# Layer norm's loads issued a block ahead, z and the attention heads stored unsplit and split after the load

## The chip, the cores and the metric

The kernel runs on one core of a Trainium2 chip. The metric is the device time of one execution in microseconds. Two runs of the kernel before took 1401.67 and 1411.05 us, median 1406.36 us.

## What is computed

One layer of a streaming encoder block for 1024 positions of width 1024, all in float32:

```python
h = rms_norm(x, g_pre)
glu_in, gate_a, q, k, v, gate_b, merge = split(h @ w_in)
u = causal_depthwise_conv31(glu_a * sigmoid(glu_b)) + conv_b
z = silu(layer_norm(u, ln_g, ln_b)) * silu(gate_a)
y_a = z @ w_conv_proj
w = softmax(q1 k1, chunk mask) - lam * softmax(q2 k2, chunk mask)   # 8 heads
o = rms_norm(w @ v, g_subln) * (1 - lambda_init)
y_b = (o * silu(gate_b)) @ w_attn_proj
y = sigmoid(m_a) * y_a + sigmoid(m_b) * y_b
out = x + rms_norm(y @ w_out, g_post)
```

A float32 product is computed from split operands: each operand is written as a high part (the value cast to the type float32r, on ScalarE, ACT) and a low part (the value less its high part, on VectorE, DVE, or GpSimd, POOL). Three matmuls, high with high, high with low and low with high, are summed in PSUM. "Splitting" below always means this cast and this subtraction.

## The kernel before

Activations lie transposed: 128 channels on the partitions, 1024 positions along the row. So a "block" is 128 x 1024 values (512 KB), and a half of it 128 x 512. Everything that a later stage needs goes through DRAM. Three stages follow one another.

**Projection.** `h @ w_in` is computed in pairs of channel blocks, each pair by seven products of halves (`quarters`, L518; `product`, L236) whose sums and differences give the four quarters of the result. The pairs and the three parts of the layer norm are ordered by hand:

```python
PLAN = ("u0 g0 u1 g1 q0 u2 q1 q2 u3 q3 q4 u4 q5 q6 u5 q7 s0 u6 s1 s2 u7 s3 v0 v1 v2 v3 "
        "m0 m1 l0 g2 l1 l2 m2 g3 m3")
```

The quarters go through up to seven buffers of the tag `cmb` (L533: `u2`, `u3`, `c22`) and six PSUM banks; the `use_` functions consume them. For the pairs m and g that is a tanh on ACT (`tanh_half`, L360) into a tile of the tag `th`, for g also a multiply, and a store. The tag `th` has six buffers (`small`, L321), used by nearly everything in this stage that has half a block.

The layer norm works on the convolved blocks in DRAM (`cv_dram`). Its parts are l0, `ln_squares` (L463): load each block, subtract the mean, store it, sum the squares; l1, `ln_roots` (L479): the inverse roots; l2, `ln_out` (L490): load each centred block (L499), multiply it by the roots (L500, DVE), silu (L501, ACT), and for each half load the gate `ga` (L504), multiply (L505, DVE), split the product (L507 ACT, L508 DVE) and store both parts (L510). Blocks lie in three buffers: two of the tag `u`, one of `cv` (`ln_tile`, L457). The halves (`gaz`, `zh`, `zl`) come from `th`.

**Attention.** Head after head (`head`, L818), in four steps of 256 queries: scores on TensorE (PE), exponentials on ACT (L859), the difference of the two maps on DVE (L868), its transposes on PE (L875), their split on ACT and DVE (L877, L878), and the product with v (L888). Between these, `take(n)` draws n pieces of other matmuls from the generator `filling` (L737): first `merge_gate` for the eight blocks of m_b (64 pieces of 6 matmuls), then `conv_out` (z @ w_conv_proj, 64 pieces of 6), then `attn_out` for the first four heads (32 pieces of 6). How many are drawn at each step is written out in `pieces` (L751). z is loaded when the gates are through (`load_z`, L671), the heads 0 to 3 ahead of `attn_out`, the heads 4 and 5 after head 6 (`load_og`, L811); both on POOL's DMA queue, into 16 block buffers which the projection's input held before (`block`, L619).

`norm_head` (L788) finishes a head: it loads the inverse roots (`orb`, L798), multiplies on POOL (L799), and splits the result (L804 ACT, L805 POOL). The heads below 6 are then stored, high and low (L809). The tiles of half a block in this stage (`orb`, `ogh`, `ogl`, `tar` and `tbr`, `yar`, `th`) share four buffers of the tag `hf` (`halftile`, L614).

**Output.** The last heads' projection, the merge, `y @ w_out` and the norm.

Within an engine and on each DMA queue instructions run in the order that the framework's scheduler fixed when the kernel was built. It goes by the program's order and by its own estimate of when operands and buffers become free. SyncE (SP) issues nearly all the DMAs; an instruction that waits there holds up those behind it.

Of the kernel before, what the change touches and what calls it, by code (L numbers as in the profile page):

```python
# [11 lines left out]
F32 = mybir.dt.float32  # L12
F32R = mybir.dt.float32r
I32 = mybir.dt.int32
AF = mybir.ActivationFunctionType
ALU = mybir.AluOpType
# [8 lines left out]
H = 8  # L25
# [42 lines left out]
def block_kernel(ctx, tc, x, positions, vecs, conv_w, lambdas, g_subln, g_post,  # L68
                 w_in, w_cp, w_ap, w_out, out):
    nc = tc.nc  # L70
# [7 lines left out]
    def rows(name, n, shape=(P, T)):  # L78
        return [dram.tile(list(shape), F32, name=f"{name}{i}") for i in range(n)]
# [4 lines left out]
    sg_dram, ga_dram, ta_dram, tb_dram = rows("sg", 8), rows("ga", 8), rows("ta", 8), rows("tb", 8)  # L84
    cc_dram = rows("cc", 8)
    b12_dram = rows("b12", 4, (P, HALF))
    cv_dram, z_dram, og_dram = rows("cv", 8), (rows("zh", 8), rows("zl", 8)), (rows("ogh", 6), rows("ogl", 6))
    ya_dram, ya2_dram = rows("ya", 8), rows("yab", 8)
    ors_dram = dram.tile([H, T], F32, name="ors_dram")

# [167 lines left out]
    for c, tiles in enumerate(((0, 1, 2, 3), (4, 5, 6, 7))):  # L258
        for t in tiles:
# [6 lines left out]
                                                        op0=ALU.mult, op1=ALU.mult)  # L266
        if c:
            begin_pair()
        for d in (range(8) if c == 0 else (4, 0, 5, 1, 6, 2, 7, 3)):
# [3 lines left out]
            g = vec[:, 0, d:d + 1]  # L273
            if c == 0 or d >= 4:
# [4 lines left out]
                                               op0=ALU.mult, op1=ALU.subtract)  # L279
# [41 lines left out]
    def small(name, dt=F32):  # L321
        return work.tile(hb, dt, name=name, tag="th", bufs=6)
# [140 lines left out]
    def ln_squares():  # L463

        mu = ps.tile(blk, F32, name="mu", tag="cv", bufs=1)
        for sl in halves:
            nc.tensor.matmul(mu[:, sl], ones_d, ln["tot"][:, sl], start=True, stop=True)
        for i in range(8):
            c = ln_tile(i, "cvr")
            nc.sync.dma_start(out=c, in_=cv_dram[i])  # L470
            nc.vector.tensor_tensor(out=c, in0=c, in1=mu, op=ALU.subtract)
            nc.sync.dma_start(out=cc_dram[i], in_=c)
            for sl in halves:
                sq = small("csq") if i else ln["tot"][:, sl]
                nc.scalar.activation(out=sq, in_=c[:, sl], func=AF.Square)
                if i:
                    nc.vector.tensor_tensor(out=ln["tot"][:, sl], in0=ln["tot"][:, sl], in1=sq, op=ALU.add)
# [12 lines left out]
    def ln_out():  # L490
        rs = ps.tile(blk, F32, name="rs", tag="cv", bufs=1)
        for a in range(8):
            dg = small("diag")[:, 0:P]
            nc.vector.tensor_scalar(out=dg, in0=ident, scalar1=ln["r"][:, a:a + 1], scalar2=float(D),
                                    op0=ALU.mult, op1=ALU.mult)
            nc.tensor.matmul(rs[:, a * P:(a + 1) * P], ones_d, dg, start=True, stop=True)
        for i in range(8):
            c = ln_tile(i, "cvz")
            nc.sync.dma_start(out=c, in_=cc_dram[i])  # L499
            nc.vector.tensor_tensor(out=c, in0=c, in1=rs, op=ALU.mult)  # L500
            nc.scalar.activation(out=c, in_=c, func=AF.Silu, scale=vec[:, 2, i:i + 1], bias=vec[:, 3, i:i + 1])  # L501
            for sl in halves:
                g = small("gaz")
                nc.sync.dma_start(out=g, in_=ga_dram[i][:, sl])  # L504
                nc.vector.scalar_tensor_tensor(out=g, in0=c[:, sl], scalar=0.5, in1=g, op0=ALU.mult, op1=ALU.mult)  # L505
                a, b = small("zh", F32R), small("zl", F32R)
                nc.scalar.copy(out=a, in_=g)  # L507
                nc.vector.tensor_tensor(out=b, in0=g, in1=a.bitcast(F32), op=ALU.subtract)  # L508
                for n, t in enumerate((a, b)):
                    nc.sync.dma_start(out=z_dram[n][i][:, sl], in_=t.bitcast(F32))  # L510

    def ln_part(n):
        (ln_squares, ln_roots, ln_out)[n]()
# [100 lines left out]
    def halftile(name="hf", dt=F32):  # L614
        return pools["h"].tile(hb, dt, name=name, tag="hf", bufs=4)
# [3 lines left out]
    def block(name):  # L619

        nblock[0] += 1
        pool, tag, n = (b2pool, "c", 4) if (nblock[0] - 1) % 16 >= 12 else (bpool, "b", 12)
        return pool.tile([P, 2, HALF], F32R, name=name, tag=tag, bufs=n).rearrange("p a b -> p (a b)")
# [44 lines left out]

    zH, zL, ogH, ogL = [], [], [], []

    def load_z(i):  # L671
        a, b = block("zH"), block("zL")
        for n, t in enumerate((a, b)):
            nc.gpsimd.dma_start(out=t.bitcast(F32), in_=z_dram[n][i])
        zH.append(a)
        zL.append(b)

    def psum_g2():
        return ps.tile(hb, F32, name="ps_g", tag="g", bufs=1)
# [39 lines left out]
    def attn_out(i):  # L719

        w = weight(("ap0", i))
        for hh in range(2):
# [11 lines left out]
                load_weight()  # L734
            yield

    def filling():  # L737
        for i in range(8):
            yield from merge_gate(i)
        for i in range(8):  # L740
            load_z(i)
        for i in range(8):
            yield from conv_out(i)
        for i in range(4):
            load_og(i)
        for i in range(8):
            yield from attn_out(i)

    fill = filling()
# [1 line left out]
    def pieces(h, i):  # L751

        if h == 3:
            return 1, int(i >= 4)
        if h == 6:
            return (0, 0) if i == 2 else (1, 1)
        return (1, 1) if h < 3 else (2, 1)
# [30 lines left out]
    def norm_head(h):  # L788

        og = heads.pop(h)  # L790
        if h >= 6:
            a, b = block("ogH"), block("ogL")
            ogH.append(a)
            ogL.append(b)
        for hh in range(2):
            sl = halves[hh]
            rb = halftile("orb")
            nc.sync.dma_start(out=rb, in_=ors_dram[h:h + 1, sl].broadcast_to([P, HALF]))  # L798
            nc.gpsimd.tensor_tensor(out=og[:, sl], in0=og[:, sl], in1=rb, op=ALU.mult)  # L799
            if h < 6:  # L800
                ah, bh = halftile("ogh", F32R), halftile("ogl", F32R)
            else:
                ah, bh = a[:, sl], b[:, sl]
            nc.scalar.copy(out=ah, in_=og[:, sl])  # L804
            (nc.vector if h == 7 else nc.gpsimd).tensor_tensor(  # L805
                out=bh, in0=og[:, sl], in1=ah.bitcast(F32), op=ALU.subtract)
            if h < 6:
                for n, t in enumerate((ah, bh)):
                    nc.sync.dma_start(out=og_dram[n][h][:, sl], in_=t.bitcast(F32))  # L809

    def load_og(h):  # L811
        a, b = block("ogH"), block("ogL")
        for n, t in enumerate((a, b)):
            nc.gpsimd.dma_start(out=t.bitcast(F32), in_=og_dram[n][h])
        ogH.append(a)
        ogL.append(b)

    def head(h, loaded_head):  # L818
        st, vH, vL, sg = loaded_head
# [93 lines left out]
    def norm_row(h):  # L913

        rt = psum_2()
        nc.tensor.transpose(out=rt[0:8, 0:P], in_=roots.pop(h), identity=ident)
        row = side("row")
        nc.scalar.copy(out=row[0:8, 0:P], in_=rt[0:8, 0:P])
        nc.sync.dma_start(out=ors_dram[h:h + 1, :].rearrange("o (a p) -> (o a) p", p=P), in_=row[0:8, 0:P])
# [8 lines left out]
    for h in range(8):  # L928
        nxt = head(h, nxt)
        if h == 6:  # L930
            load_og(4)
            load_og(5)
    norm_row(7)
    norm_head(7)
    for _ in fill:
# [152 lines left out]
```

## Time and profile before

| | |
|---|---|
| Two runs, median | 1401.67 and 1411.05, 1406.36 us |
| The profiled execution, its own time | 1409.51 us |
| Its span, first to last instruction | 1407.4 us |
| Mean granted clock of TensorE | 0.942 |
| Moved by DMA | 237.89 MB |

A row of the tables by stretches gives the start and end in us, the length, the busy us of PE, PEld (weight load), DVE, ACT and POOL with the number of instructions, then TensorE's granted clock, the share of DMA that was busy, and GB/s. A row of a timeline gives start, length, engine, line, operation, the tile written and those read, the shape, the count, and in brackets how long the engine was idle before and what ended this. SPq is SyncE's DMA queue, POOLq GpSimd's. A row of waits gives who waited for whom, the us in total, how often, and the longest. A row of one line's or tile's instructions gives count, shortest, median and longest in ns, and the first and last start. A row of DMA issues ends with the size of each and the median us from issue to landing.

### The profile page before, as it was taken

Reading aid. Unit: us, or ns where it says so; the run is one execution under the profiler, and the core shown is the slowest. Engines: PE = TensorE matmul, PEld = TensorE weight load, DVE = VectorE, ACT = ScalarE, POOL = GpSimd, SP = SyncE. Lnnn points to the kernel's source line nnn. Section 1 sums busy time; section 2 is a strip of 40 time slices with the busy share of each in tenths; the row PEclk is TensorE's granted clock in tenths of the full one; section 3 lists DMA queues with packets and bytes.
Section 4 is the critical chain, followed back from the end, with each engine's and each line's share of the span. In section 5 each row is a group of like instructions: output and inputs, shape, how many; then the busy total and the mean of one; then the engine's idle time right before and its main releaser. Section 6 shows DMA issues by size and latency. Waiting matters only on the chain. (4 is left out here: it accounts for less than half of the span.)

```text
span 1407.4 us, 17086 instructions
## 1 busy us (share of the span) xinstructions
PE 1221.7 (87%) x5700; PEld 1009.3 (72%) x5700; DVE 990.4 (70%) x1561; ACT 528.8 (38%) x1051; POOL 698.1 (50%) x560
## 2 busy tenths in 40 slices
PE   3799999999899999998921699988899889969998
PEld 2578777878788877786810488877778778857786
DVE  4879998998999999639533165676566567836733
ACT  7533342323333333343422254544343335423311
POOL 4798799999888886675500211322221223353000
PEclk9999999999999999999965699998999999989999
DMA  5223444434432244655456956688756676558432
GB/s 206 71 85 110 150 142 157 155 118 154 149 120 91 93 169 142 232 170 200 139 182 214 236 158 182 179 256 284 219 175 195 173 241 205 191 189 266 155 121 86
DMA packets 100279, 237.89 MB, mean 169 GB/s; under 512 B 12016, under 2 KB 12480, under 8 KB 100192
## 3 DMA queue, kind: packets, MB, share of 16 engines
q1 hardware_dynamic: 95360, 219.75, 49.6%
q0 software_dynamic: 4112, 14.83, 2.9%
q10 hardware_dynamic: 720, 2.23, 0.4%
q8 instruction: 45, 0.74, 0.2%
q14 instruction: 42, 0.34, 0.1%
HBM read 157.04 MB, written 79.72 MB: 168 GB/s over the span
## 5 line engine op out<-in xcount | busy, mean ns | idle before, releaser
L241 PE MATMUL ps_g<-T,wf 128*128 128x512 f32 x1536 | 362.3, 392 | 5.8 <-DVE u L525 5.6
L241 PE MATMUL ps_g<-B,wf 128*128 128x512 f32 x1152 | 289.9, 405 | 74.9 <-DVE c L525 70.2
L241 PEld LDWEIGHTS ps_g<-T,wf 128*128 128x128 f32 x1536 | 289.3, 189 | 67.6 <-DVE u L525 5.2
L241 PEld LDWEIGHTS ps_g<-B,wf 128*128 128x128 f32 x1152 | 224.3, 196 | 126.9 <-DVE c L525 73.9
L447 DVE SCALAR_TENSOR_TENSOR cacc<-u,cw,cacc 128x1024 f32<-128x1024 f32 x232 | 297.7, 1283 | 2.9
L182 POOL TENSOR_TENSOR wf<-wraw,wf 128x512 fp32r<-128x512 f32 x128 | 177.4, 1390 | 56.7 <-ACT wf L181 56.7
L644 POOL TENSOR_TENSOR wL<-wraw,wH 128x512 fp32r<-128x512 f32 x44 | 57.8, 1328 | 271.3 <-ACT wH L643 252.5
L182 POOL TENSOR_TENSOR wf<-wsum,wf 128x512 fp32r<-128x512 f32 x96 | 130.0, 1354 | 23.1 <-ACT wf L181 22.8
L859 ACT ACTIVATE e<-ps_s,nm 128x256 f32<-128x256 f32 (+7 forms) x128 | 94.7, 743 | 97.4 <-DVE nm L856 36.4
L181 ACT CAST wf<-wraw 128x512 fp32r<-128x512 f32 x128 | 78.2, 617 | 98.3 <-PE ps_g L241 80.5
L709 PE MATMUL ps_g<-B,wH 128*128 128x512 f32 x256 | 87.4, 423 | 18.5 <-ACT wH L643 13.2
L181 ACT CAST wf<-wsum 128x512 fp32r<-128x512 f32 x96 | 59.3, 618 | 87.5 <-POOL wsum L203 44.4
L525 DVE SCALAR_TENSOR_TENSOR u<-ps_g,u 128x512 f32<-128x512 f32 x96 | 65.6, 684 | 37.3 <-PE ps_g L241 37.1
L846 PE MATMUL ps_s<-kst,qh 128*128 128x384 f32 (+4 forms) x192 | 69.5, 370 | 5.8 <-ACT e L859 5.8
L878 DVE TENSOR_TENSOR wtL<-ps_r,wtH 128x512 fp32r<-128x512 f32 (+2 forms) x96 | 52.1, 549 | 30.3 <-ACT wtH L877 29.8
L709 PEld LDWEIGHTS ps_g<-B,wH 128*128 128x128 f32 x256 | 50.8, 204 | 30.4 <-ACT wH L643 13.9
L847 PE MATMUL ps_s<-kst,ql 128*128 128x384 f32 (+4 forms) x192 | 66.5, 354 | 1.0 <-DMA ql<-qkl 1.0
L856 DVE TENSOR_REDUCE nm<-ps_s 128x1 f32<-128x640 f32 (+3 forms) x64 | 65.1, 1018 | 0.9
L799 POOL TENSOR_TENSOR og<-og,orb 128x512 f32<-128x512 f32 x16 | 20.5, 1281 | 84.6 <-DMA orb<-ors_dram 59.2
L666 PE MATMUL ps_g<-zH,wH 128*128 128x512 f32 x128 | 53.2, 416 | 9.5 <-DVE tar L692 9.5
L203 POOL TENSOR_TENSOR wsum<-wraw 128x512 f32<-128x512 f32 x32 | 43.7, 1365 | 35.9 <-DMA wraw<-w_in 33.6
L877 ACT CAST wtH<-ps_r 128x512 fp32r<-128x512 f32 (+2 forms) x96 | 44.7, 479 | 39.5 <-PE ps_r L875 39.0
(227 smaller groups left out, 2360.4 us busy)
## 6 DMA issues: line engine op xcount, KB each, us to landing
wraw<-w_in SPq DMA_DIRECT2D x67, 512.0 KB, 3.7
qkh<-qkH SPq DMA_DIRECT2D x32, 256.0 KB, 2.3
qkl<-qkL SPq DMA_DIRECT2D x32, 256.0 KB, 2.0
qh<-qkh SPq DMA_DIRECT2D x32, 256.0 KB, 7.8
ql<-qkl SPq DMA_DIRECT2D x32, 256.0 KB, 8.4
tbr<-tb SPq DMA_DIRECT2D x32, 256.0 KB, 2.9
sg<-th SPq DMA_DIRECT2D x16, 256.0 KB, 5.0
cv<-cv SPq DMA_DIRECT2D x8, 512.0 KB, 4.0
```

Source lines behind the costliest of these rows:

```text
L181: nc.scalar.copy(out=f[:, 0, :], in_=src)
L182: nc.gpsimd.tensor_tensor(out=f[:, 1, :], in0=src, in1=f.bitcast(F32)[:, 0, :], op=ALU.subtract)
L241: nc.tensor.matmul(acc, f[:, l, sl], b[:, r, :], start=(start and d + n == 0), stop=False, skip_group_check=True)
L447: nc.vector.scalar_tensor_tensor(out=a if k == TAPS - 1 else acc, in0=u[:, k:k + T], scalar=cw[:, i, k:k + 1], in1=acc, op0=ALU.mult, op1= ...
L525: nc.vector.scalar_tensor_tensor(out=out, in0=acc, scalar=pos if s is None else s, in1=u, op0=ALU.mult, op1=ALU.add)
L644: (eng or nc.gpsimd).tensor_tensor(out=wL[:, sl], in0=raw, in1=wH.bitcast(F32)[:, sl], op=ALU.subtract)
L666: nc.tensor.matmul(acc, w[l][:, sl], rhs[r][d][:, halves[hh]], start=(d - first + n == 0), stop=(d == last and n == 2))
L709: nc.tensor.matmul(acc, w[l][:, sl], f[:, r, :], start=(d + n == 0), stop=(d == 7 and n == 2))
L846: nc.tensor.matmul(sv[:, a, :], qh[:, qs], k[:, ks], start=True, stop=False)
L847: nc.tensor.matmul(sv[:, a, :], ql[:, qs], k[:, ks], start=False, stop=True)
L856: nc.vector.tensor_reduce(out=nm[:, m:m + 1], in_=sv, op=ALU.max, axis=AX.XY, negate=True)
L859: nc.scalar.activation(out=e[:, :n].rearrange("p (a b) -> p a b", a=c), in_=sv, func=AF.Exp, bias=nm[:, m:m + 1], accum_out=Z[:, i, m:m + 1])
```

## The change

Three things are changed.

1. `ln_squares` and `ln_out` load a block ahead: blocks 0 and 1 before the loop, block i+1 at the top of turn i (from turn 1 on); in `ln_out` the two gate halves are loaded with the block.
2. z and the heads 0 to 5 are stored once, unsplit. `ln_out` multiplies the gate into the block's own buffer and stores the whole block; `norm_head` stores the halves of `og` for heads below 6.
3. The parts are made after the load. `load_raw2` loads the raw block into the buffer of the low part; `split_raw` casts it into the high part's buffer (ACT) and subtracts in place (POOL), by halves. `split_first` spreads this over the filling: a first call that only issues the loads, two calls that split two blocks each, and the remaining blocks behind the first pieces of `conv_out(0)` or `attn_out(0)`. Heads 4 and 5 are split after head 7. `pieces` now draws a second piece in the first four steps of head 3 too.

```diff
-    cv_dram, z_dram, og_dram = rows("cv", 8), (rows("zh", 8), rows("zl", 8)), (rows("ogh", 6), rows("ogl", 6))
+    cv_dram, z_dram, og_dram = rows("cv", 8), rows("zd", 8), rows("ogd", 6)
...
-        for i in range(8):
+        def load(i):
             c = ln_tile(i, "cvr")
             nc.sync.dma_start(out=c, in_=cv_dram[i])
+            return c
+
+        cs = [load(0), load(1)]
+        for i in range(8):
+            if 0 < i < 7:
+                cs.append(load(i + 1))
+            c = cs[i]
             nc.vector.tensor_tensor(out=c, in0=c, in1=mu, op=ALU.subtract)
             nc.sync.dma_start(out=cc_dram[i], in_=c)
...
-        for i in range(8):
+        def load(i):
             c = ln_tile(i, "cvz")
             nc.sync.dma_start(out=c, in_=cc_dram[i])
+            gs = [small("gaz") for _ in halves]
+            for g, sl in zip(gs, halves):
+                nc.sync.dma_start(out=g, in_=ga_dram[i][:, sl])
+            return c, gs
+
+        cs = [load(0), load(1)]
+        for i in range(8):
+            if 0 < i < 7:
+                cs.append(load(i + 1))
+            c, gs = cs[i]
             nc.vector.tensor_tensor(out=c, in0=c, in1=rs, op=ALU.mult)
             nc.scalar.activation(out=c, in_=c, func=AF.Silu, scale=vec[:, 2, i:i + 1], bias=vec[:, 3, i:i + 1])
-            for sl in halves:
-                g = small("gaz")
-                nc.sync.dma_start(out=g, in_=ga_dram[i][:, sl])
-                nc.vector.scalar_tensor_tensor(out=g, in0=c[:, sl], scalar=0.5, in1=g, op0=ALU.mult, op1=ALU.mult)
-                a, b = small("zh", F32R), small("zl", F32R)
-                nc.scalar.copy(out=a, in_=g)
-                nc.vector.tensor_tensor(out=b, in0=g, in1=a.bitcast(F32), op=ALU.subtract)
-                for n, t in enumerate((a, b)):
-                    nc.sync.dma_start(out=z_dram[n][i][:, sl], in_=t.bitcast(F32))
+            for g, sl in zip(gs, halves):
+                nc.vector.scalar_tensor_tensor(out=c[:, sl], in0=c[:, sl], scalar=0.5, in1=g, op0=ALU.mult, op1=ALU.mult)
+            nc.sync.dma_start(out=z_dram[i], in_=c)
...
-    def load_z(i):
-        a, b = block("zH"), block("zL")
-        for n, t in enumerate((a, b)):
-            nc.gpsimd.dma_start(out=t.bitcast(F32), in_=z_dram[n][i])
-        zH.append(a)
-        zL.append(b)
+    def load_raw2(src, names, H, L, i):
+
+        a, b = block(names[0]), block(names[1])
+        nc.gpsimd.dma_start(out=b.bitcast(F32), in_=src[i])
+        H.append(a)
+        L.append(b)
+
+    def split_raw(a, b):
+
+        for sl in halves:
+            nc.scalar.copy(out=a[:, sl], in_=b.bitcast(F32)[:, sl])
+            nc.gpsimd.tensor_tensor(out=b[:, sl], in0=b.bitcast(F32)[:, sl], in1=a.bitcast(F32)[:, sl],
+                                    op=ALU.subtract)
...
+    def split_first(gen, H, L, n):
+
+        yield
+        d = 0
+        for _ in range(2):
+            for d in (d, d + 1):
+                split_raw(H[d], L[d])
+            d += 1
+            yield
+        for _ in gen:
+            for _ in range(2):
+                if d < n:
+                    split_raw(H[d], L[d])
+                    d += 1
+            yield
+
     def filling():
         for i in range(8):
             yield from merge_gate(i)
         for i in range(8):
-            load_z(i)
-        for i in range(8):
+            load_raw2(z_dram, ("zH", "zL"), zH, zL, i)
+        yield from split_first(conv_out(0), zH, zL, 8)
+        for i in range(1, 8):
             yield from conv_out(i)
         for i in range(4):
             load_og(i)
-        for i in range(8):
+        yield from split_first(attn_out(0), ogH, ogL, 4)
+        for i in range(1, 8):
             yield from attn_out(i)
...
         if h == 3:
-            return 1, int(i >= 4)
+            return 1, 1
...
             if h < 6:
-                ah, bh = halftile("ogh", F32R), halftile("ogl", F32R)
+                nc.sync.dma_start(out=og_dram[h][:, sl], in_=og[:, sl])
             else:
-                ah, bh = a[:, sl], b[:, sl]
-            nc.scalar.copy(out=ah, in_=og[:, sl])
-            (nc.vector if h == 7 else nc.gpsimd).tensor_tensor(
-                out=bh, in0=og[:, sl], in1=ah.bitcast(F32), op=ALU.subtract)
-            if h < 6:
-                for n, t in enumerate((ah, bh)):
-                    nc.sync.dma_start(out=og_dram[n][h][:, sl], in_=t.bitcast(F32))
+                nc.scalar.copy(out=a[:, sl], in_=og[:, sl])
+                (nc.vector if h == 7 else nc.gpsimd).tensor_tensor(
+                    out=b[:, sl], in0=og[:, sl], in1=a.bitcast(F32)[:, sl], op=ALU.subtract)
...
     def load_og(h):
-        a, b = block("ogH"), block("ogL")
-        for n, t in enumerate((a, b)):
-            nc.gpsimd.dma_start(out=t.bitcast(F32), in_=og_dram[n][h])
-        ogH.append(a)
-        ogL.append(b)
+        load_raw2(og_dram, ("ogH", "ogL"), ogH, ogL, h)
...
+    for d in (4, 5):
+        split_raw(ogH[d], ogL[d])
     norm_row(7)
     norm_head(7)
```

## The prediction, made before the change was run

> **What bounds the kernel now.** I read the page first, for where TensorE (PE) is not busy.
>
> ```profile
> span 1407.4 us, 17086 instructions
> PE 1221.7 (87%) x5700; PEld 1009.3 (72%) x5700; DVE 990.4 (70%) x1561; ACT 528.8 (38%) x1051; POOL 698.1 (50%) x560
> PE   3799999999899999998921699988899889969998
> PEclk9999999999999999999965699998999999989999
> ```
>
> The span is 1407.4 us; this execution's own time is 1409.5 us. PE is at nine tenths nearly everywhere, so elsewhere an idle engine costs nothing. The exception is slices 21 and 22 (a slice is 35 us), where PE falls to 2 and 1 tenths. The table by stretches cuts that place finely, and the waits of 560 to 800 us name it.
>
> ```profile
> 584.00:647.00 63.00, 59.05 (x265) 48.23 (x263) 33.56 (x38) 28.70 (x51) 39.64 (x30) 1.00 0.64 222
> 672.50:712.30 39.80, 39.72 (x176) 32.52 (x174) 22.30 (x27) 15.61 (x23) 17.31 (x13) 1.00 0.49 159
> 712.30:764.70 52.40, 0.00 (x0) 0.00 (x0) 17.36 (x24) 11.55 (x18) 0.00 (x0) 0.55 0.51 165
> 764.70:774.20 9.50, 4.69 (x12) 3.40 (x12) 3.90 (x6) 4.87 (x8) 0.00 (x0) 0.68 1.06 367
> 803.00:1262.00 459.00, 415.43 (x2209) 353.05 (x2208) 289.38 (x718) 193.22 (x461) 123.41 (x113) 0.95 0.68 205
> PE ps_g L241 <- DVE c L525: 55.2, 2, 52.5
> ```
>
> After the stretch come its length and the busy time of PE, PEld, DVE, ACT and POOL. From 672.5 to 712.3 PE runs without a hole. Then it does nothing for 52.4 us, while DVE is busy only 17.4 us and DMA half busy: no engine is the limit, a chain is. The timeline shows its links: a turn of `ln_out`'s inner loop, the last matmuls before the hole, and its end.
>
> ```profile
> 742.14 0.42 SPq L504 DMA_DIRECT2D gaz<-ga  x1
> 745.27 0.69 DVE L505 SCALAR_TENSOR_TENSOR gaz<-cvz,gaz 128x512 f32<-128x512 f32 x1 [2.80 <-DMA gaz<-ga]
> 746.03 0.62 ACT L507 CAST zh<-gaz 128x512 fp32r<-128x512 f32 x1 [4.30 <-DVE gaz L505]
> 746.68 0.32 SPq L510 DMA_DIRECT2D zh<-zh  x1
> 747.05 0.42 SPq L504 DMA_DIRECT2D gaz<-ga  x1
> ...
> 709.34 2.88 PE L241 MATMUL ps_g<-T,wf 128*128 128x512 f32 x12
> ...
> 762.45 0.62 ACT L362 ACTIVATE th<-c 128x512 f32<-128x512 f32 x1
> 764.00 0.69 DVE L525 SCALAR_TENSOR_TENSOR c<-ps_g,u 128x512 f32<-128x512 f32 x1
> 764.74 4.69 PE L241 MATMUL ps_g<-B,wf 128*128 128x512 f32 x12 [52.52 <-DVE c L525]
> ```
>
> Each load of `gaz` is issued 0.37 us behind the store of the half before: load, multiply, cast, store, next load, about 5 us a half, never two loads in flight. The first tanh (L362) that stores the projections m2, g3 and m3 comes at 762.45, after the last half. These tanh tiles share the six buffers of tag `th` with `ln_out`. Until they drain, the seven combination buffers (`cmb`) and PSUM stay full, as I read the code; the `c` of L525 gets its place 1.5 us after that tanh, and PE resumes. So the stage ends with `ln_out`, though PE had only 12 matmuls left at 712.
>
> **The change, part by part.**
>
> 1. *Loads a block ahead, no zh and zl.* The durations:
>
> ```profile
> L500 DVE TENSOR_TENSOR cvz<-cvz,rs x8: 1214/1220/1222, 672.6 to 733.8; 128x1024 f32<-128x1024 f32 x8
> L501 ACT ACTIVATE cvz<-cvz,vec x8: 1232/1242/1247, 673.8 to 735.0; 128x1024 f32<-128x1024 f32 x8
> L505 DVE SCALAR_TENSOR_TENSOR gaz<-cvz,gaz x16: 682/692/835, 676.6 to 761.1; 128x512 f32<-128x512 f32 x16
> cc<-cvr SPq DMA_DIRECT2D x8, 512.0 KB, 2.9
> cvz<-cc SPq DMA_DIRECT2D x8, 512.0 KB, 3.9
> cv<-cv SPq DMA_DIRECT2D x8, 512.0 KB, 4.0
> zL<-zl POOLq DMA_DIRECT2D x8, 512.0 KB, 8.3
> ogL<-ogl POOLq DMA_DIRECT2D x6, 512.0 KB, 11.2
> ```
>
> Today the eight blocks start 61.2 us apart over seven steps (672.6 to 733.8), 8.7 us each, and the last halves trail to 761. Afterwards the limit is the ring of three block buffers: z is stored from the block's own buffer, so block i+3 can load only when z of block i has landed. A turn is a store of 512 KB (2.9 to 4.0, by the `cc` and `cv` stores; I take 4.0), the load 3.9, multiply 1.22, silu 1.24, two half multiplies 1.38 and about 0.5 of issue: 12.2 us for three blocks. Block 0 ends at about 676.5 (672.6 plus 1.22, 1.24, 1.38), block 6 two turns later at 701, block 7 at 703, and its store lands at 707. That is before 712.3, where PE would first need it. The 16 `gaz` loads no longer alternate with zh and zl in the tag's order, so six can be under way; the tag is free for the tanh tiles from about block 5 on, near 695. PE then runs through: minus 52.5 us. The last 12 matmuls take 2.9 instead of 4.7 us since PE hasn't idled (granted clock 0.55 and 0.68 in those two stretches against 1.00): minus 1.8. For instructions that DVE's fixed order still puts behind a late load I add back 2 us (0 to 20; the upper end is rival one). The removed 16 casts and 16 subtractions lie inside this hole and earn nothing more. The loads ahead in `ln_squares` I cost at nothing: PE covers that stretch with 59.05 of 63 us. Without that cover they could win these two holes, 6.4 us at most:
>
> ```profile
> 643.88 3.03 PE L241 MATMUL ps_g<-B,wf 128*128 128x512 f32 x12 [2.69 <-DVE c L525]
> 664.10 2.93 PE L496 MATMUL rs<-diag,ones_d 128*128 128x128 f32 x12 [3.68 <-DVE diag L494]
> ```
>
> What is late next is the stage's own tail: the last tanh stores, then the attention stage's loads. It follows PE's last matmul as before and only moves forward.
>
> 2. *Heads stored unsplit.* `ogh` and `ogl` leave the four `hf` buffers, which `tar`, `orb`, `tbr` and `yar` share.
>
> ```profile
> 1048.87 0.53 SPq L809 DMA_DIRECT2D ogh<-ogh  x1
> 1049.51 0.38 SPq L686 DMA_DIRECT2D tar<-ta  x1
> ...
> PE ps_g L666 <- DVE tar L692: 9.5, 2, 5.9
> ```
>
> The two stalls in which the projection waits for `tar` (9.5 us in all) both follow a `tar` load issued behind a head's `ogh` store. Without these tiles the loads can come earlier, but `orb` still takes buffers: bounds 0 and minus 9.5; I take minus 6.
>
> 3. *Splitting in the attention stage.* There z costs 16 casts and 16 POOL subtractions that stage did not have; those of the heads only move from storing to reading. POOL issues 14 loads in place of 28.
>
> ```profile
> L804 ACT CAST ogh<-og x12: 617/620/630, 889.4 to 1180.5; 128x512 fp32r<-128x512 f32 x12
> L805 POOL TENSOR_TENSOR ogl<-og,ogh x12: 1262/1282/1498, 890.1 to 1181.2; 128x512 fp32r<-128x512 f32 x12
> L814 POOL DMA_DIRECT2D ogH<-ogh x6: 527/528/574, 1145.6 to 1183.7; - x6
> 1080.28 5.50 PE ps_g L666 x24
> ```
>
> ACT: 16 x 0.62 = 9.9 us onto 193 of 459 us. POOL: 16 x 1.28 = 20.5 less 14 x 0.53 = 7.4, so plus 13 onto 123. Neither is the bound; PE covers them with 415 of 459 us. Behind a cast on ACT wait the exponentials and the `wtH` casts, and PE behind those: 0 to 9.9 us; I take 4. Behind a POOL subtraction waits a DVE instruction now and then:
>
> ```profile
> 925.83 2.68 POOL L644 TENSOR_TENSOR wL<-wraw,wH 128x512 fp32r<-128x512 f32 x2 [16.89 <-ACT wH L643]
> 926.00 1.27 DVE L157 TENSOR_TENSOR ry<-ry,rq 128x8 f32<-128x8 f32 x1
> 930.31 0.17 DVE L157 TENSOR_TENSOR ry<-ry,rq 128x8 f32<-128x8 f32 x1
> ```
>
> The same small DVE instruction takes 0.17 us alone and 1.27 beside a POOL subtraction. Sixteen new subtractions could each cost 1.1: 0 to 17.6 us. DVE is busy 63% of the stage, and only some of its instructions are of this kind; I take 3. The Trainium skill, SBUF — State Buffer, section "Who interferes with whom", speaks against this part of the change: GpSimd reads through a port that DVE needs for a second operand in SBUF, and the second to come is blocked for the whole instruction. By it the subtraction moved from DVE to POOL isn't free even with POOL idle, and the sum would be the lock rival's below; the trace agrees with the lock, at 1.27 against 0.17.
>
> Six calls of the filling now bring no matmuls (three for z, three for the heads). A call is 6 matmuls, 5.50 / 4 = 1.4 us of cover: 0 to 8.2 us in all; head 3 asks for four more calls, so none are lost; I take 3. Heads 4 and 5 are split after head 7 in the program; I cost it at nothing, since their loads (the last block begins at 1183.7) land by about 1195 (11.2 later) and POOL is idle for most of the stage; if they came last, four subtractions, 5.1 us, would stand before head 7's. The halved traffic I also credit nothing.
>
> **Sum**: -52.5 - 1.8 + 2 - 6 + 4 + 3 + 3 = -48.3. Against the profiled 1409.5 that gives 1361.2. The median of the two runs shown is 1406.4, and 1358.1 is what I forecast on that basis.
>
> **The rivals.**
>
> *One: `ln_out` still ends the stage* (0.07). If SP, in order, keeps each load behind a store that waits for its block, a block costs load 3.9 + 1.22 + 1.24 + 1.38 + 0.7 issue = 8.4 us; eight from 672.6 end at 740, the store at 744, against 720 for PE's tail: 24 more, 1382. For it: SP waits in order in the rows above. Against: the loads now stand ahead of those stores in the program.
>
> *Two: ACT waits for the raw loads* (0.07). A cast that stands too early in ACT's order stops the exponentials until the load lands. The loads come in three groups (z in two, as buffers free up, and the heads), 8.3 + 8.3 + 11.2 = 27.8 us where all are exposed: 1358.1 + 27.8 - 4 = 1382. Against: the split comes a call or more after the loads.
>
> *The lock* (0.05): all sixteen collide, 17.6 - 3 more: 1372.7.
>
> *Loads not really ahead* (0.04): if the scheduled queue still puts each `gaz` load behind the former block's work, the hole remains; the costs of part 3 (10) less 6 are left: 1410.
>
> *Slower* (0.03): ACT meets each of the 14 raw loads separately, 8 x 8.3 + 6 x 11.2 = 133.6 us: 1358.1 + 133.6 - 4 = 1488. It decides from the sixth exposed load on (52.3 us won before ACT's waits, about 9.5 each). Against: the loads are issued side by side.
>
> **How the numbers follow.** The forecast has 0.74. Down: all small costs at zero (12), the rest of `tar` (3.5) and the two holes (6.4) give 1336; I end at 1338. Up: rivals one and two, and the lock, end at 1382; I take 1384. What lies outside is a little over a tenth. A measurement tells about 2% (28 us, so 1378) from no change. Faster by over 2%: 0.74, the lock's 0.05 and half of rivals one and two (they spread around the bound), 0.86. Within 2%: the other half and the loads not ahead, 0.11. Slower: 0.03.
>
> **What would show it.** PE's hole of 52 us is below 10, its twelve matmuls take 2.9 us, the first tanh of m2 comes near 695, and the `L500` starts span about 30 us. The `tar` wait is under 4. The waits of ACT for raw loads stay under 10 in total. I am wrong if PE still idles over 15 us waiting for `c`, or if the attention stage grows by more than 15 us.

## The result and the profile after

The changed kernel took 1345.22 us (1344.42 and 1346.01) against 1406.36 us: a ratio of 0.9565, 95% interval 0.9426 to 0.9704, so 61 us less. The forecast was 1358.1, its range 1338 to 1384. Two executions further below, one of before and one of z_sub_dve, ran at a clock of 0.65 and 0.66 and took some 380 us longer; they are left out of the times, and the latter is the only profile of z_sub_dve, so that only its time is used.

The page of the changed kernel, in the order of the rows shown of before:

```profile
span 1342.6 us, 16960 instructions
PE 1208.9 (90%) x5700; PEld 1002.6 (75%) x5700; DVE 992.9 (74%) x1545; ACT 526.7 (39%) x1051; POOL 711.7 (53%) x562
PE   3899998999899999999795899979999978978997
PEclk9899999999899999999897899998999979989999
```

No slice but the first is below 5 tenths. The table by stretches, cut at the end of the projection, and the waits of 660 to 780 us:

```profile
672.50:716.10 43.60, 43.50 (x194) 35.73 (x192) 35.93 (x40) 21.89 (x30) 19.16 (x13) 1.00 0.74 265
716.10:728.60 12.50, 0.00 (x0) 0.00 (x0) 0.63 (x1) 2.18 (x4) 0.00 (x0) 0.60 1.04 296
PE ps_g L727 <- ACT wH L654: 12.6, 1, 12.6
```

PE now runs without a hole to the end of the projection at 716; the wait of 52.5 us for the tile `c` is gone from the list. What follows is the change to the attention stage (12.6 us now, 13.2 before), which only moved forward. `ln_out` and PE's end in the timeline and in the rows of the tile `cvz` (L517 is the old L500, L520 the old L505, L521 the store of z):

```profile
L517 DVE TENSOR_TENSOR cvz<-cvz,rs x8: 1203/1220/1222, 673.6 to 710.4; 128x1024 f32<-128x1024 f32 x8
L521 SPq DMA_DIRECT2D zd<-cvz x8: 319/320/462, 680.3 to 714.3; - x8
666.40 1.74 SPq L509 DMA_DIRECT2D gaz<-ga  x4
701.10 0.64 ACT L362 ACTIVATE th<-c 128x512 f32<-128x512 f32 x1 [1.82 <-DVE cvz L520]
713.12 2.88 PE L241 MATMUL ps_g<-B,wf 128*128 128x512 f32 x12
```

Four gate loads are issued within 1.74 us; before, each stood alone. The eight blocks start within 36.8 us (61.2 before), the first tanh behind them comes at 701 (762 before), and PE's last 12 matmuls take 2.88 us. But the last store of z is issued at 714.3, PE's last matmuls at 713.1: `ln_out` fits in front of PE's end with nothing to spare.

The attention stage is measured below from the first matmul of the merge gates to the first of the heads' last projection (`ps_o` from `ogH`). Before and after, by the rows of these two lines and the table by stretches:

```profile
L709 PE MATMUL ps_g<-B,wH x256: 387/389/797, 782.6 to 968.5; 128*128 128x512 f32 x128
L666 PE MATMUL ps_o<-ogH,wH x64: 389/389/793, 1259.7 to 1309.9; 128*128 128x512 f32 x64
782.60:1259.70 477.10, 428.59 (x2249) 362.98 (x2249) 289.84 (x720) 196.81 (x467) 129.17 (x118) 0.94 0.69 205
```

```profile
L727 PE MATMUL ps_g<-B,wH x256: 387/389/796, 728.6 to 894.5; 128*128 128x512 f32 x128
L677 PE MATMUL ps_o<-ogH,wH x64: 389/389/797, 1193.3 to 1244.2; 128*128 128x512 f32 x64
728.60:1193.30 464.70, 419.34 (x2248) 357.44 (x2248) 298.11 (x720) 203.14 (x483) 144.58 (x119) 0.95 0.65 189
```

The stage starts 54.0 us earlier (782.6 to 728.6) and is some 12 us shorter besides, though 16 casts and 16 subtractions came to it. The merge gates end after 166 us instead of 186. The prediction had this stage 4 us longer. So two questions were left: what opened the hole (loads written ahead, or the tiles zh and zl gone), and where the attention stage won 12 us.

### The profile page after: what moved, and what is told of

Same layout as the page of the kernel before. It is cut to its first block, busy times and chain, and to the rows that moved or that the text cites. A ratio compares the mean times of both kernels' runs of the same rounds, so it can differ in the third digit from the quotient of the medians.

```text
span 1342.6 us, 16960 instructions
## 1 busy us (share of the span) xinstructions
PE 1208.9 (90%) x5700; PEld 1002.6 (75%) x5700; DVE 992.9 (74%) x1545; ACT 526.7 (39%) x1051; POOL 711.7 (53%) x562
## 5 line engine op out<-in xcount | busy, mean ns | idle before, releaser
L727 PE MATMUL ps_g<-B,wH 128*128 128x512 f32 x256 | 84.9, 411 | 16.6 <-ACT wH L654 12.6
L727 PEld LDWEIGHTS ps_g<-B,wH 128*128 128x128 f32 x256 | 49.4, 197 | 28.5 <-ACT wH L654 13.0
L203 POOL TENSOR_TENSOR wsum<-wraw 128x512 f32<-128x512 f32 x32 | 42.9, 1341 | 35.7 <-DMA wraw<-w_in 33.6
L677 PE MATMUL ps_g<-zH,wH 128*128 128x512 f32 x128 | 52.8, 412 | 8.4 <-DVE tar L710 4.5
L896 DVE SCALAR_TENSOR_TENSOR e<-e,rz 128x128 f32<-128x128 f32 (+3 forms) x64 | 56.1, 876 | 1.1
```

The source lines that it names most:

```text
L677: nc.tensor.matmul(acc, w[l][:, sl], rhs[r][d][:, halves[hh]], start=(d - first + n == 0), stop=(d == last and n == 2))
L727: nc.tensor.matmul(acc, w[l][:, sl], f[:, r, :], start=(d + n == 0), stop=(d == 7 and n == 2))
```

## The experiments

Each ratio is against the kernel before on the same chip. "Hole", "gates" and "stage" are of one profile each: PE's wait for `c`, the time from the first gate matmul to the last, and the time to the first of the heads' last projection (from unrounded starts).

| kernel | us | ratio, 95% interval | hole | gates | stage |
|---|---|---|---|---|---|
| before | 1406.36 | 1 | 52.5 | 186 | 477.0 |
| changed | 1345.22 | 0.9565, 0.9426 to 0.9704 | none | 166 | 464.7 |
| ahead_split | 1383.98 | 0.9863, 0.9819 to 0.9906 | 21.2 | 187 | 480.1 |
| raw_in_turn | 1346.86 | 0.9597, 0.9558 to 0.9635 | none | 169 | 467.3 |
| th_order | 1372.58 | 0.9755, 0.9717 to 0.9793 | 25.6 | 167 | 462.8 |
| heads_split | 1352.73 | 0.9639, 0.9596 to 0.9683 | none | 184 | 470.0 |
| pieces_old | 1348.02 | 0.9603, 0.9560 to 0.9646 | none | 169 | 472.0 |
| hf_order | 1356.17 | 0.9650, 0.9616 to 0.9684 | none | 182 | 474.8 |
| heads_raw | 1385.42 | 0.9855, 0.9824 to 0.9886 | 53.5 | 162 | 450.0 |
| sub_dve | 1340.63 | 0.9537, 0.9509 to 0.9565 | none | 166 | 453.6 |
| after_again | 1347.07 | 0.9591, 0.9564 to 0.9618 | none | 166 | 465.0 |
| sub_dve_again | 1337.29 | 0.9529, 0.9504 to 0.9554 | none | 169 | 460.1 |
| no_z_sub | 1334.91 | 0.9523, 0.9488 to 0.9558 | none | 167 | 453.1 |
| z_sub_dve | 1340.96 | 0.9549, 0.9522 to 0.9576 | only the time is used | | |

The stage of one kernel varied by 0.3 us between two profiles (changed, after_again) and by 6.5 between two others (sub_dve): a difference under about 7 us in that column settles nothing by itself.

### What opened the hole

**ahead_split**: loads ahead and nothing else.

```diff
-            for sl in halves:
-                g = small("gaz")
-                nc.sync.dma_start(out=g, in_=ga_dram[i][:, sl])
+            for g, sl in zip(gs, halves):
...
                 a, b = small("zh", F32R), small("zl", F32R)
```

> The kernel before with the layer norm's loads a block ahead and nothing else: z and heads are stored split as before. Theory (the order of the tag th: a load could not be issued before the low part of the half ahead of it had its buffer, so one load was in flight at a time): with the gate halves of a block allocated ahead of zh and zl of the block before, two to four loads are in flight, the hole of 52 us shrinks below 20 us, time about 1360 to 1385. Rival (the zh and zl tiles and their stores fill the buffers, going ahead does nothing): hole 45 us or more, time 1398 to 1410.

Measured: 1383.98 us and a hole of 21.2 us. The rival (45 us or more) is out, and the theory's "below 20" is missed by a little. The gate loads now come in pairs, but zh and zl still stand between the pairs; the blocks start over 42.6 us.

```profile
L517 DVE TENSOR_TENSOR cvz<-cvz,rs x8: 1203/1219/1223, 671.2 to 713.8; 128x1024 f32<-128x1024 f32 x8
734.15 2.08 PE L241 MATMUL ps_g<-B,wf 128*128 128x512 f32 x4 [21.16 <-DVE c L540]
```

**raw_in_turn**: z unsplit, every load in its own turn.

```diff
-        cs = [load(0), load(1)]
-        for i in range(8):
-            if 0 < i < 7:
-                cs.append(load(i + 1))
-            c, gs = cs[i]
+        for i in range(8):
+            c, gs = load(i)
```

> The changed kernel with both layer norm loops loading each block in its own turn. Theory (the order of the tag): without zh and zl nothing stands between two loads in the tag, the scheduler moves them forward by itself, the hole stays below 10 us and the time within 8 us of the changed kernel's 1345. Rival (the loads written ahead are what wins): the loads stand behind the stores again, about 4 us of load per block on the chain, hole 20 us or more, time 1365 to 1395.

Measured: 1346.86 us, no hole, within 2 us of the changed kernel. The rows of its blocks and stores are those of the changed kernel to within a microsecond, and its first four gate loads go out together too:

```profile
666.33 1.75 SPq L506 DMA_DIRECT2D gaz<-ga  x4
L511 DVE TENSOR_TENSOR cvz<-cvz,rs x8: 1205/1220/1222, 672.9 to 710.3; 128x1024 f32<-128x1024 f32 x8
L515 SPq DMA_DIRECT2D zd<-cvz x8: 319/320/427, 680.2 to 714.2; - x8
```

So writing the loads a block ahead, which names the change, does nothing that these runs show once zh and zl are gone: the scheduler had moved the loads forward by itself.

**th_order**: the buffers' order without the traffic. The loads stand in turn, and each half takes two more tiles of `th`, with one column in each.

```diff
+                a, b = small("zh"), small("zl")
+                nc.scalar.copy(out=a[:, 0:1], in_=c[:, sl][:, 0:1])
+                nc.vector.tensor_tensor(out=b[:, 0:1], in0=c[:, sl][:, 0:1], in1=a[:, 0:1], op=ALU.subtract)
```

> The changed kernel (z stored unsplit, as a block) with the gate halves loaded in turn and, between two of them, two more tiles of the tag th that hold one column each and are not stored. They add about 0.4 us of work a half and no traffic. Theory (a tile of a tag takes its buffer in the program's order, so a load can't be issued before the small subtraction of the half ahead of it): one gate load in flight again, some 5 us a half, the hole is back at 30 us or more and the time at 1375 to 1400. Rival (what held the layer norm back were the 32 stores of zh and zl and the full casts and subtractions): hole below 10 us, time 1344 to 1354.

Measured: 1372.58 us, a hole of 25.6 us. The rival (under 10 us) is out: with the stores and the full casts gone, the two small tiles of a half still make half of the old hole. The theory asked for 30 us or more and 1375 or above, and missed by a little. The timeline shows the loads one by one again, about 2.9 us behind one another within a block (L515), and then the store of the block (L520). In SyncE's queue the second gate load stands behind a block load (L506), which waits there until a store of z has landed (in all 10.2 us in five waits):

```profile
709.88 0.32 SPq L520 DMA_DIRECT2D zd<-cvz  x1
710.24 0.43 SPq L515 DMA_DIRECT2D gaz<-ga  x1
712.77 0.32 SPq L506 DMA_DIRECT2D cvz<-cc  x1
713.13 0.43 SPq L515 DMA_DIRECT2D gaz<-ga  x1
718.01 0.32 SPq L520 DMA_DIRECT2D zd<-cvz  x1
718.37 0.43 SPq L515 DMA_DIRECT2D gaz<-ga  x1
```

A block takes 8.1 us here (709.88 to 718.01), against 11.7 before (722.1 to 733.8, L500). The difference goes with the full casts, subtractions and stores, which th_order leaves out. One thing is not separated: each pair of small tiles also brings a copy and a subtraction, which take their places in the fixed orders of ACT and DVE. The same two instructions into tiles of another tag were not run, so it is likely, but not shown by itself, that the order of the buffers does it and not that of these instructions.

### Where the attention stage won

**heads_raw**: the kernel before with the heads' part alone (stored unsplit, split after the load, pieces of head 3 as in the change); the layer norm and z as before.

```diff
             if h < 6:
-                ah, bh = halftile("ogh", F32R), halftile("ogl", F32R)
+                nc.sync.dma_start(out=og_dram[h][:, sl], in_=og[:, sl])
```

> The kernel before with the heads' part of the change and the pieces of head 3 alone: heads stored unsplit, split after the load; the layer norm and z as before. Its hole of 52 us stays. Theory (most of the 12 us of the attention stage belong to the heads' part): the stage from the first merge gate to the last projection falls from 477 to 470 us or less, time 1393 to 1400. Rival (they belong to z's part): 475 us or more, time 1403 to 1410.

Measured: 1385.42 us, 21 us less than before though the hole of 53.5 us stays; the stage falls to 450.0. That is 27 us less than before, far more than the theory asked, and 15 us less than in the changed kernel.

```profile
L716 PE MATMUL ps_g<-B,wH x256: 387/389/796, 783.5 to 945.4; 128*128 128x512 f32 x128
783.50:1233.50 450.00, 414.41 (x2249) 353.55 (x2249) 298.84 (x722) 197.30 (x471) 129.23 (x112) 0.97 0.71 206
```

**hf_order** (the buffers' order without the traffic) and **heads_split** (the heads' part undone in the changed kernel):

```diff
             if h < 6:
+                ah, bh = halftile("ogh"), halftile("ogl")
+                nc.scalar.copy(out=ah[:, 0:1], in_=og[:, sl][:, 0:1])
+                nc.gpsimd.tensor_tensor(out=bh[:, 0:1], in0=og[:, sl][:, 0:1], in1=ah[:, 0:1], op=ALU.subtract)
                 nc.sync.dma_start(out=og_dram[h][:, sl], in_=og[:, sl])
```

> The changed kernel with two more tiles of the tag hf for each half of the heads 0 to 5, one column each, not stored; the heads are still stored unsplit. Theory (the order of the tag hf held the gates and tar back): the stage from the first merge gate to the last projection of the heads (465 us in the changed kernel, 477 before) becomes 3 to 10 us longer, time 1348 to 1356. Rival (the traffic of the split heads, 12 more stores and 6 more loads, was the cost): no change, 1343 to 1348.

> The changed kernel with the heads stored split again, in tiles of the tag hf, and loaded as two parts. Theory (the unforeseen 12 us in the attention stage come from the hf buffers: late tar loads stop TensorE and are each followed by some 7 us at half clock): the waits for tar return, 6 us or more together, and the time is 8 to 16 us above the changed kernel, about 1353 to 1361. Rival (the gain there comes from the four more pieces in head 3 or from z's traffic): within 4 us of 1345.

Measured: hf_order 1356.17 us, its stage 10.1 us longer than the changed kernel's; heads_split 1352.73, 5.3 longer. hf_order lies outside its rival's 1343 to 1348, at the upper end of its theory; its interval (0.9616 to 0.9684) and the changed kernel's (0.9564 to 0.9618, after_again) only just touch. heads_split lies above its rival's 1349, but its interval (0.9596 to 0.9683) overlaps the changed kernel's further, so its size is open. And the mechanism written into the theory of heads_split fell: no wait for `tar` came back in it. What did come back in both is the late end of the gates, 182 and 184 us after their start. All kernels with the tiles ogh and ogl in the tag `hf` stand at 182 to 187, even with one column and no traffic; all without, at 162 to 169. The first kind has one long gap between two gate matmuls: 28.5 us in before, 28.0 in ahead_split, 24.4 in heads_split, 21.7 in hf_order; heads_raw and the changed kernel have none over 12. The trace of before shows what stands in it, in the ACT and PE rows around head 2's norm:

```profile
933.22 0.39 PE L709 MATMUL ps_g<-B,wL 128*128 128x512 f32 x1
...
959.54 0.62 ACT L804 CAST ogh<-og 128x512 fp32r<-128x512 f32 x1 [3.12 <-POOL og L799]
961.11 0.59 ACT L713 ACTIVATE th<-ps_g 128x512 f32<-128x512 f32 x1
961.75 0.50 PE L709 MATMUL ps_g<-B,wH 128*128 128x512 f32 x1 [0.68 <-ACT th L713]
```

The tanh tile of a merge gate is of the tag `hf` too, and comes behind head 2's `ogh` and `ogl`. The second `ogh` is cast at 959.54, after ACT had stood idle for it (3.12 us, behind POOL's multiply); then the gate's tanh empties the only PSUM bank that the filling has, and the gate's matmuls, still since 933.6, go on at 961.75. Here too the buffers and ACT's fixed order are not separated: in hf_order the tanh (897.77) likewise stands behind the one-column copy to the second `ogh` (896.94), for which ACT waited 3.87 us.

**pieces_old**: the pieces of head 3 as before.

```diff
         if h == 3:
-            return 1, 1
+            return 1, int(i >= 4)
```

> The changed kernel with the pieces of head 3 drawn as before (one instead of two in its first four steps). Theory (hf buffers): 0 to 6 us slower, 1345 to 1351: four pieces, 5.5 us of matmuls, are left for the end of the stage with nothing beside them. Rival (the pieces drawn early are what shortened the attention stage): 10 us or more slower, 1355 or above.

Measured: 1348.02 us, a stage of 472.0. The time is in the theory's band and the rival's 1355 isn't reached: by the time, the four early pieces won little. The stage is 7.3 us longer than the changed kernel's, about as much as that column can tell.

**The two parts do not add.** The table has all four combinations of the two parts (before, heads_raw, heads_split, changed; heads_split draws head 3's pieces as the change does), and the worth of each depends on the other. Beside z split before its store, the heads' part takes 27 us off the stage (477.0 to 450.0); beside z split after the load, it takes 5.3 (470.0 in heads_split to 464.7), by the times some 6 to 8 us. In the same way z's part lengthens the stage by 15 us beside unsplit heads (450.0 to 464.7), but not beside split ones (470.0, against 477.0 before and 480.1 in ahead_split). So the 12 us are what the two do together, and the account below by way of heads_raw is one of two.

### What z's split costs in the attention stage

heads_raw (z split before its store) has a stage 15 us shorter than the changed kernel. **sub_dve** (and sub_dve_again), **z_sub_dve** and **no_z_sub** ask which of the new work that is.

```diff
-            nc.gpsimd.tensor_tensor(out=b[:, sl], in0=b.bitcast(F32)[:, sl], in1=a.bitcast(F32)[:, sl],
+            nc.vector.tensor_tensor(out=b[:, sl], in0=b.bitcast(F32)[:, sl], in1=a.bitcast(F32)[:, sl],
                                     op=ALU.subtract)
```

> The changed kernel with the subtractions of split_raw on VectorE instead of GpSimd (28 of them, 0.69 instead of 1.28 us each). If the shared port between GpSimd and VectorE costs what the prediction set aside for it (3 us), the time falls by 0 to 4 us, to 1341 to 1345; if VectorE is what the attention heads wait for, it rises by 3 us or more, to 1348 or above.

> The changed kernel with all 28 subtractions of split_raw on VectorE once more: 1339 to 1342, 3 to 7 us below the changed kernel on the same chip, if that gain is no accident of the chip; within 2 us of it if it is.

> The changed kernel with only z's 16 subtractions on VectorE; those of the heads stay on GpSimd. Theory (GpSimd's subtractions of z hold up VectorE's instructions with two operands in SBUF, and themselves take 1.28 instead of 0.69 us): most of the 11 us that the stage gained with all 28 on VectorE are here, the stage from the first gate to the last projection lasts 452 to 459 us, time 1338 to 1343. Rival (it was the 12 of the heads): 463 us or more, 1344 to 1348.

> The changed kernel with z's 16 subtractions left out (the low part keeps the raw value). Theory (the subtractions on GpSimd are z's cost in the attention stage): as with them on VectorE or a little less, stage 450 to 457 us, time 1336 to 1342. Rival (the 16 casts on ACT, the raw loads and the three calls without matmuls are z's cost): stage 461 us or more, 1343 to 1347.

> The changed kernel once more, on the same chip as the two kernels beside it: 1343 to 1348, stage 463 to 468 us. Both theories need it as the measure.

Measured: sub_dve 1340.63 us (1341 to 1345 expected for the shared port), and on another chip 1337.29 (below the 1339 expected) beside 1347.07 of the changed kernel; the two intervals there (0.9504 to 0.9554, 0.9564 to 0.9618) do not touch. z_sub_dve took 1340.96, in its theory's band, but its interval (0.9522 to 0.9576) overlaps both of these, so how much of the gain is z's is open. With z's subtractions left out the time is 1334.91 (its theory began at 1336; interval 0.9488 to 0.9558) and the stage lasts 453.1, 12 us less than after_again. The stretches of the stage, after_again, sub_dve_again and no_z_sub:

```profile
725.90:1190.90 465.00, 420.07 (x2249) 358.04 (x2249) 296.84 (x720) 202.75 (x483) 144.89 (x119) 0.95 0.65 189
```

```profile
729.10:1189.10 460.00, 419.34 (x2248) 358.33 (x2248) 304.01 (x748) 203.22 (x483) 108.51 (x91) 0.95 0.66 191
```

```profile
726.90:1180.00 453.10, 418.52 (x2248) 357.39 (x2248) 290.79 (x720) 202.99 (x483) 124.49 (x103) 0.95 0.66 194
```

Moving 28 subtractions takes 36 us off GpSimd (144.89 to 108.51) and brings 28 x 0.69 = 19.3 us of work to VectorE, yet VectorE is busy only 7.2 us longer (296.84 to 304.01): its other instructions got 12.1 us shorter. That is what the Trainium skill, SBUF — State Buffer, section "Who interferes with whom", says of a VectorE instruction with two operands in SBUF beside a GpSimd instruction that reads SBUF, and the trace agrees by these 12.1 us.

Compared instruction by instruction, 9.3 of the 12.1 us lie where the heads are split (1065 to 1120 us in after_again) and 2.7 where z is (865 to 915). In no_z_sub VectorE's own 720 instructions lose 6.05 us (296.84 to 290.79), and of these too only 3.3 lie where z is split: 4.4 are a single instruction of L926, of two columns, beside subtractions of the heads, which that kernel keeps. In the profile of the changed kernel:

```profile
L926 DVE SCALAR_TENSOR_TENSOR zz<-Z x32: 132/153/7176, 756.5 to 1160.6; 128x2 f32<-128x2 f32 x32
1107.06 2.54 POOL L693 TENSOR_TENSOR ogL<-ogL,ogH 128x512 fp32r<-128x512 f32 x2
1107.32 7.18 DVE L926 SCALAR_TENSOR_TENSOR zz<-Z 128x2 f32<-128x2 f32 x1
1109.56 1.26 POOL L655 TENSOR_TENSOR wL<-wraw,wH 128x512 fp32r<-128x512 f32 x1
1110.79 1.25 POOL L749 TENSOR_TENSOR tbr<-tbr,yar 128x512 f32<-128x512 f32 x1
1112.00 2.47 POOL L693 TENSOR_TENSOR ogL<-ogL,ogH 128x512 fp32r<-128x512 f32 x2
1114.73 1.11 PE L903 MATMUL ps_r<-ident,e 128*128 128x128 f32 x4 [4.80 <-DVE var L927]
```

Its median is 0.15 us; this one takes 7.18. GpSimd runs six instructions without a pause from 1107.06 to 1114.47, VectorE's ends at 1114.50, and PE waits 4.8 us for what follows it. It is 5.13 us in after_again, 6.93 in raw_in_turn, 7.69 in th_order and 3.25 in hf_order, and at most 1.25 in the other profiles here, so part of the differences between stages is whether this one collision happens.

Of the 12 us by which no_z_sub's stage is shorter, 8 are there at the first scores matmul of head 4 (216.1 us into the stage, 224.2 in after_again); the other 4 come later, where z is no longer split. Of the 8, VectorE's 3.3 us and the chain from the cast to the matmul, which also lost 1.28 us per half, were not separated.

Of the versions that compute everything sub_dve has the lowest times, 1337 to 1341 us, ratios 0.9529 and 0.9537 against before; z_sub_dve's interval overlaps its own.

## Why the prediction was right, and where it was not

**Part 1, the hole.** Forecast -52.5 - 1.8 + 2 = -52.3; the last projection matmul came at 769.0 before and 715.6 after: -53.4. Right in size, and in mechanism as far as the runs show it: zh and zl between two loads of a tag, with th_order's small tiles making half of the hole, and their casts, subtractions and stores going with the other half. Two of its readings were too good. The ring of three block buffers gave 36.8 us from the first to the last block, not about 30, so the first tanh came at 701, not 695, and z's last store at 714.3, not 703. It still fitted before PE's end at 716, but the five microseconds that the prediction saw between them (707 and 712.3) were not there. And the loads *written* ahead were not the cause (raw_in_turn).

**Part 2, the heads.** "Bounds 0 and minus 9.5; I take minus 6." The `tar` stalls that it priced did fall, from 9.5 to 4.5 us (`PE ps_g L677 <- DVE tar L710: 4.5, 3, 2.1`), though not under the 4 that it named as a sign. But with z as before, the heads' part alone shortened the stage by 27 us (heads_raw, 477.0 to 450.0) and the kernel by 21; with z's part in place it shortened the stage by 5.3, near the 6. The prediction priced the parts as if they added. And it followed the tag `hf` only to the tile that a row of waits named, `tar`. It counted `tar`, `orb`, `tbr` and `yar` as users of the four buffers and left out `th`, the merge gates' tanh, which stood behind the heads' tiles as well. PE's row of waits could not show that: PE had other matmuls in its fixed order, and the gate's wait appears as 0.68 us where 28 us passed. How the 27 us divide was not settled: hf_order's small tiles brought 10.1 back, and the rest may be traffic, or the fixed order as a whole, which every edit changes.

**Part 3, splitting in the attention stage.** Forecast 4 + 3 + 3 = 10; heads_raw to the changed kernel gives 14.7. The two are not quite the same sum, since three of the six empty calls are in heads_raw already. The subtractions were set at 3: VectorE does lose 3.3 us where z is split, but the stage is 12 us shorter without z's subtractions. These 12 lie within the bounds given to the lock (0 to 17.6), but the lock is not shown to be all of them. Casts, raw loads and empty calls, set at 7, have 3 us left at the end of the stage; at head 4's first scores matmul, which heads_raw reaches 207.4 us into the stage, they still have 9. So this share is not settled either. What the prediction put at nothing are the heads' subtractions, which "only move from storing to reading": where they now stand they held the one instruction of L926 for 7.18 us, and PE for 4.8.

**The rest.** The pause between the projection and the attention stage is 0.6 us shorter (13.0 after 13.6); the output stage starts 66.3 us earlier and its last matmul ends 65.0 earlier, so it is 1.3 longer. So -53.4 - 27.0 + 14.7 - 0.6 + 1.3 = -65.0; the two spans differ by 64.8. Parts 2 and 3 together were forecast at +4 and came out at -12.3. That is nearly all of the 16.5 us by which the spans went further than the forecast (48.3); by the medians it is 12.8. That the errors of the two parts, 21 us too little gain and 5 too little cost, by way of heads_raw, partly cancel is luck.

**The rivals.** One (the layer norm still ends the stage) came close: the two ends lie a microsecond apart. Two: ACT waited 15.7 us for raw loads (11.1 for the heads, 4.6 for z), over the 10 that I allowed, but no kernel here shows a price for it. The lock came true in part, but most of it at the heads' subtractions and not at the sixteen of z that the rival counted. Loads not ahead and slower did not happen.

```profile
ACT ogH L692 <- DMA ogL<-ogd: 11.1, 3, 7.3
ACT zH L692 <- DMA zL<-zd: 4.6, 2, 3.9
```

## What to carry to other kernels

Two tiles of one column in a shared tag, with their two small instructions and no traffic, were enough to bring back a hole of 25.6 us (th_order) or to hold the merge gates for 21.7 us (hf_order). List all users of a tag before pricing one of them. A shorter tile list can do what rewriting the loop does (raw_in_turn): the scheduler then moves the loads by itself. The parts of a change need not add: the heads' part was worth 27 us of the stage or 5.3, by what stood beside it. Moving an elementwise subtraction to an idle GpSimd was not free here while VectorE read two operands from SBUF, least of all several in a row.

## What the runs showed that I had not expected

A stall of PE can cost more than its length. Around the second `tar` stall of before, four stretches with the granted clock in the third column from the end, and a matmul of the same shape from each of the last two:

```profile
1108.00:1115.00 7.00, 7.00 (x40) 5.98 (x38) 3.82 (x9) 3.20 (x9) 2.79 (x2) 1.00 1.03 236
1115.00:1121.00 6.00, 0.26 (x2) 0.06 (x1) 0.54 (x1) 0.00 (x0) 0.00 (x0) 0.91 1.04 298
1121.00:1126.50 5.50, 5.30 (x13) 4.14 (x14) 4.40 (x10) 1.55 (x4) 0.00 (x0) 0.50 1.06 279
1126.50:1133.00 6.50, 6.50 (x43) 5.93 (x42) 2.16 (x7) 2.48 (x7) 0.94 (x1) 0.98 0.97 185
1123.08 0.63 PE L666 MATMUL ps_g<-zL,wH 128*128 128x512 f32 x1
1127.08 0.40 PE L666 MATMUL ps_g<-zH,wL 128*128 128x512 f32 x1
```

In the 5.5 us behind the stall the clock is 0.50 and a matmul of 128x512 takes 0.63 us, after it 0.40. In heads_raw the stage's 2249 matmuls keep PE busy for 414.4 us at a mean clock of 0.97, before for 428.6 at 0.94: of the 27 us, 14 are the same matmuls running faster, and 13 are idle time. The prediction counted the cold clock behind the hole (1.8 us), but not behind the small stalls.
